# Two-layer hybrid diffusion step on one Trainium2 core: the instruction order made by the scheduler's detailed timeline instead of its plain one

## The chip, the cores and the metric

One core of one Trainium2 chip runs the whole program. The metric is device time in microseconds (us), as the median of several runs. Engines are named as in the profile: PE (TensorE), PEld (its weight load), DVE (VectorE), ACT (ScalarE), POOL (GpSimd), SP (SyncE, which issues most transfers).

## What is computed

Two layers (DEPTH = 2), width D = 2048, on 128 context and 128 latent tokens. Cut to what matters, one layer is:

```
m = adaLN(c)                      # shift, scale, gate: 2 x 3 vectors, from ada_w
h = norm(x) * scale + shift
u = h @ w_in                      # one product for all three head groups
oA = windowed attention(u)        # 12 heads, sink, context keys
oB = Hyena convolution by FFT(u)
oC = RWKV-7, forward and backward(u)   # 12 heads, decay, delta rule, chunked
x = x + gate * norm([oA, oB, oC] @ w_out)
h = norm(x) * scale' + shift'
x = x + gate' * norm(relu(h @ w1)^2 @ w2)
```

Weights are fp32. Each one is split into a high and a low part, and a product is three matmuls (high x high, low x high, high x low).

## The kernel before

**The main work** streams weights. `wload` (L208) issues a transfer on SP (L218), ACT casts the high part (L219), DVE subtracts for the low part (L220). `ws` (L482) then issues matmuls 256 columns wide (L495, L498, L499), and `as_` (L505) matmuls 512 columns wide (L514, L517, L518; 256 wide for the attention values). The input product is `ws` for RWKV and Hyena and `as_` for attention; the output product `w_out` is `as_`; the MLP uses both.

**The modulation work** ("ADA" below) makes the adaLN vectors: transfer L369, small matmuls L374, 16 to a piece. The first vectors are made in a boot stretch (L329 to L344), the others between main products.

**The side work** of the mixer is written as generators that the main loops advance (`Side`, L130): attention, Hyena, and RWKV in two batches (0 and 1) of three blocks of two heads each. For one batch the steps follow one another:

1. `rwkv_stage1` (L803): per block a transpose of the values (L814), small products (L820 to L850), transposes (L880), 32 matmuls of line L904, products L914 to L925, transposes L933, whose result POOL stores (L938).
2. `rwkv_invert` (L947): eight loads on SP of the stored matrices (L956, tile rX), a triangular inversion on DVE of 30 steps (L964, L965), a copy and a store (L971, L977).
3. `rwkv_stage2` (L981): loads the inverse (L985), then seven half-steps of 24 small matmuls each (L1003, L1001, L1003, ...), each followed by an L1007 pair on DVE, or by an L1009 copy on DVE and an L1011 copy on ACT; then L1018 to L1027.
4. `rwkv_out` (L1033): group norm and output transposes (L1061).

**What sets the order.** The program's own order is a priority. A scheduler of the library then puts the instructions of each engine into the order in which they go on the chip; it simulates when an instruction could start. In the kernel before it uses its plain timeline. Every engine runs its list in that fixed order: an instruction that isn't ready holds up all behind it on its engine. `w_out` runs in three phases over the heads (L1098 on), attention's and Hyena's heads first, RWKV's batch 0 and then batch 1 last. So the mixer ends with: batch 1's chain, the last phase, the residual and the norm (L1205).

## Time and profile before

| | |
|---|---|
| median of 3 runs | 2949.42 us (2944.27 to 2960.29) |
| profiled execution, its own time | 2948.62 us |
| its span | 2946.8 us |
| PE busy | 2833.7 us (96%) |
| PEld, DVE, ACT, POOL busy | 79%, 56%, 42%, 6% |
| bytes moved | 654.56 MB, mean 222 GB/s |
| boot; mixer 0; MLP 0; mixer 1; MLP 1 begin at about | 0; 140; 770; 1620; 2210 us |

PE is busy nearly all the time. What is left to win or lose is the time in which PE waits, and the time in which it runs at the lower of its two clocks: busy time there counts as busy too, so the granted clock (1.00 is 2.4 GHz, 0.50 is 1.2 GHz) must be read beside it. Stretches are therefore read one by one, not by the average.

### The profile page before, as it was taken

To read this page: it belongs to the slowest core of one execution; us is meant where nothing else is said; L and a number is where in the kernel's file an instruction comes from. 1 tells how busy PE (TensorE), PEld (TensorE's weight loads), DVE (VectorE), ACT (ScalarE), POOL (GpSimd) and SP (SyncE) were. 2 spreads that over 40 slices of the span, in tenths; PEclk is the share of its full clock that TensorE was granted. 3 is DMA by queue.
4 is the path that set the end of the run, shared out by engine and by line. 5 is a ranking of instruction groups with operands and counts; after the bars stand their busy time and mean duration, and the time that the engine had idled before them with its cause. 6 is when DMAs were issued, how large, how long until landed. Compare 5 with 4: busy or idle time off the path is not lost.

```text
span 2946.8 us, 47852 instructions
## 1 busy us (share of the span) xinstructions
PE 2833.7 (96%) x19163; PEld 2318.8 (79%) x19163; DVE 1651.4 (56%) x2627; ACT 1230.8 (42%) x1870; POOL 177.5 (6%) x368
## 2 busy tenths in 40 slices
PE   6899999999899999999999999999879999999998
PEld 2586787767797797897876978887669989889896
DVE  1356666776654344444446576776775545545555
ACT  2354345434543343343335454453355444444343
POOL 0011101201000000000000111011000000000000
PEclk9999899999999999999999998998889999999999
DMA  9985575477888888888898744533455666666674
GB/s 337 333 296 185 188 253 157 137 258 275 296 280 288 275 287 274 299 283 281 284 334 274 232 135 114 147 93 95 138 189 170 188 187 186 186 187 186 188 240 150
DMA packets 326057, 654.56 MB, mean 222 GB/s; under 512 B 48581, under 2 KB 86030, under 8 KB 325707
## 3 DMA queue, kind: packets, MB, share of 16 engines
q1 hardware_dynamic: 311328, 610.88, 64.0%
q0 software_dynamic: 12928, 36.98, 3.8%
q10 hardware_dynamic: 1579, 3.64, 0.3%
q8 instruction: 150, 2.46, 0.3%
q14 instruction: 72, 0.59, 0.1%
HBM read 632.21 MB, written 19.20 MB: 221 GB/s over the span
## 4 chain that ended last, share of the span: by engine, by line
PE 86%; DVE 5%; DMA 5%; ACT 2%; issue 1%; SPq 0%; POOL 0%; DVEq 0%; ACTq 0%; POOLq 0%
PE mm L495 12%; PE mm L499 12%; PE mm L498 12%; PE mm L514 11%; PE mm L517 11%; PE mm L518 11%; PE ada L374 5%; PE sm L904 2%; DMA wa<-in_ada_w_dram 2%; PE sm L925 1%; PE sm L1003 1%; DVE wl L220 1%; PE sm L1018 1%; PE sm L1001 1%; DMA wr<-in_ada_w_dram 1%
## 5 line engine op out<-in xcount | busy, mean ns | idle before, releaser
L220 DVE TENSOR_TENSOR wl<-wr,wh 128x1024 fp32r<-128x1024 f32 (+1 forms) x784 | 928.1, 1185 | 931.2 <-ACT wh L219 910.0
L219 ACT CAST wh<-wr 128x1024 fp32r<-128x1024 f32 (+1 forms) x784 | 796.5, 1017 | 1169.3 <-PE mm L498 545.6
L495 PE MATMUL mm<-acth,wh 128*128 128x256 f32 (+1 forms) x3200 | 914.4, 286 | 11.5 <-ACT acth L476 9.2
L499 PE MATMUL mm<-acth,wl 128*128 128x256 f32 (+1 forms) x3200 | 907.1, 283 | 2.4 <-DVE wl L220 2.4
L498 PE MATMUL mm<-actl,wh 128*128 128x256 f32 (+1 forms) x3200 | 907.5, 284 | 0.3 <-DVE actl L477 0.3
L495 PEld LDWEIGHTS mm<-acth,wh 128*128 128x128 f32 (+1 forms) x3200 | 605.2, 189 | 56.3 <-issue 23.8
L499 PEld LDWEIGHTS mm<-acth,wl 128*128 128x128 f32 (+1 forms) x3200 | 605.2, 189 | 8.3 <-DVE wl L220 3.4
L498 PEld LDWEIGHTS mm<-actl,wh 128*128 128x128 f32 (+1 forms) x3200 | 605.4, 189 | 3.9 <-issue 2.5
L517 PE MATMUL mm<-wl,fh 128*128 128x512 f32 x1024 | 408.0, 398 | 0.3 <-DVE wl L220 0.3
L514 PE MATMUL mm<-wh,fh 128*128 128x512 f32 x1024 | 406.6, 397 | 0.0
L518 PE MATMUL mm<-wh,fl 128*128 128x512 f32 x1024 | 402.4, 393 | 0.0
L514 PEld LDWEIGHTS mm<-wh,fh 128*128 128x128 f32 x1024 | 191.8, 187 | 67.6 <-ACT wh L219 10.9
L518 PEld LDWEIGHTS mm<-wh,fl 128*128 128x128 f32 x1024 | 192.3, 188 | 45.7
L517 PEld LDWEIGHTS mm<-wl,fh 128*128 128x128 f32 x1024 | 192.4, 188 | 43.8 <-DVE wl L220 0.8
L374 PE MATMUL ada<-wa,cs 128*32 128x512 f32 x1280 | 180.6, 605 | 9.2 <-DMA wa<-in_ada_w_dram 9.1
L514 PE MATMUL mm<-wh,osh 128*128 128x512 f32 x256 | 108.8, 425 | 3.4 <-ACT osh L1172 3.4
L517 PE MATMUL mm<-wl,osh 128*128 128x512 f32 x256 | 105.0, 410 | 3.4 <-DVE wl L220 3.4
L518 PE MATMUL mm<-wh,osl 128*128 128x512 f32 x256 | 103.0, 402 | 0.0
L374 PEld LDWEIGHTS ada<-wa,cs 128*32 128x32 f32 x1280 | 35.3, 109 | 84.9 <-issue 54.2
L904 PE MATMUL sm<-rZR,rKB 64*128 64x256 f32 x384 | 83.8, 456 | 0.7 <-DVE rLA L908 0.3
L514 PE MATMUL mm<-wh,acth 128*128 128x512 f32 (+1 forms) x192 | 74.8, 389 | 0.0
L517 PE MATMUL mm<-wl,acth 128*128 128x512 f32 (+1 forms) x192 | 69.1, 360 | 0.0
(323 smaller groups left out, 2598.2 us busy)
## 6 DMA issues: line engine op xcount, KB each, us to landing
wr<-in_mlp_w_dram SPq DMA_DIRECT2D x512, 512.0 KB
wa<-in_ada_w_dram SPq DMA_DIRECT2D x352, 512.0 KB
wr<-in_w_in_dram SPq DMA_DIRECT2D x96, 512.0 KB
wr<-in_w_in_dram SPq DMA_DIRECT2D x112, 384.0 KB
wr<-in_w_out_dram SPq DMA_DIRECT2D x64, 512.0 KB
wr<-in_ada_w_dram SPq DMA_DIRECT2D x32, 512.0 KB
gb<-gate POOLq DMA_DIRECT2D x16, 512.0 KB, 8.9
xd<-acc SPq DMA_DIRECT2D x24, 256.0 KB
```

Of the source, the lines that this page charges most:

```text
L219: nc.scalar.copy(hi, raw)
L220: nc.vector.tensor_sub(lo, raw, hi)
L374: nc.tensor.matmul(ps[32 * j:32 * j + 32, :], lhsT=self.cs[:, kk, :], rhs=w[2 * (kk - k + 1) + j // 2][:, 512 * (j % 2):512 * (j % 2) + 51 ...
L495: m = nc.tensor.matmul(o, lhsT=h, rhs=hh, start=(k == 0 and b % 2 == 0), stop=False, skip_group_check=True)
L498: nc.tensor.matmul(o, lhsT=h, rhs=hl, start=False, stop=False, skip_group_check=True)
L499: nc.tensor.matmul(o, lhsT=lw, rhs=hh, start=False, stop=(k == KT - 1), skip_group_check=True)
L514: m = nc.tensor.matmul(o, lhsT=hh, rhs=hi[:, kk, :], start=first, stop=False)
L517: nc.tensor.matmul(o, lhsT=hh, rhs=lo[:, kk, :], start=False, stop=False)
L518: nc.tensor.matmul(o, lhsT=hl, rhs=hi[:, kk, :], start=False, stop=last)
L904: nc.tensor.matmul(ps[h][:, i * 256:(i + 1) * 256], lhsT=KB[hs, d, g, i, :], rhs=ZR[hs, d, g, :, :].rearrange("p i t -> p (i t)"), start=T ...
L925: nc.tensor.matmul(o[:, 64 * h:64 * h + 64], lhsT=R.MA[d][h][:, 0:128] if i == 0 else MY[h][:], rhs=vT[:, g, 64 * h:64 * h + 64], start=fi ...
L1001: nc.tensor.matmul(o, lhsT=LA[d][:, gh, qs[d]], rhs=G[:, d, gh, :], start=True, stop=True)
```

## The change

The context that holds the scheduler is opened with a flag: the scheduler then times the instructions with its detailed timeline of engines and DMAs. Nothing else is edited.

```
-    with _tile.TileContext(nc) as tc:
+    with _tile.TileContext(nc, schedule_with_timeline_sim=True) as tc:
```

Every engine has the same compute instructions before and after; their order differs in the boot, in both mixers and in the residual between, and is the same on PE in both MLPs. On PE 2748 of 15617 rows of the order move. In the rows below a name is a tile (the number is its instance), `<-` stands before what is read, and `x2` counts equal neighbours. The three places are these.

**PE, layer 1, RWKV batch 1, from the first block to the second in stage 1.** The tiles `mm` are of the main input product. Before:

```order
L814 MATMUL sm_19059<-const_66,ru_v_17922 128x128 x2
L499 MATMUL mm_19097<-acth_14714,wl_19100 128x256
L495 MATMUL mm_19097<-acth_14714,wh_19099 128x256
L820 MATMUL sm_19064<-rtw_15195,rup_18776 128x256 x2
L828 MATMUL sm_19071<-rad_15196,rup_18778 128x256 x2
L845 MATMUL sm_19124<-rinv_2844_18774,const_66 128x256
L850 MATMUL sm_19128<-rrk_19057,const_66 128x256
L498 MATMUL mm_19097<-actl_14715,wh_19099 128x256
L499 MATMUL mm_19097<-acth_14714,wl_19100 128x256
L495 MATMUL mm_19097<-acth_14714,wh_19099 128x256
```

Now:

```order
L814 MATMUL sm_19059<-const_66,ru_v_17922 128x128 x2
L925 MATMUL sm_19011<-rvT_18785,rMY_19008 128x64
L820 MATMUL sm_19064<-rtw_15195,rup_18776 128x256 x2
L828 MATMUL sm_19071<-rad_15196,rup_18778 128x256 x2
L845 MATMUL sm_19124<-rinv_2844_18774,const_66 128x256
L850 MATMUL sm_19128<-rrk_19057,const_66 128x256
L880 MATMUL sm_19181<-const_66,rkf_19155 128x128 x2
L904 MATMUL sm_19212<-rZR_19149,rKB_19150 128x256
L904 MATMUL sm_19213<-rZR_19149,rKB_19150 128x256
```

The main matmuls that stood between the small ones of this block have all gone ahead of it; the three blocks of this batch now follow each other with no main matmul between.

**DVE, layer 1, the start of the first inversion.** L708 to L718 are attention's softmax, tile rX is what the inversion works on. Before:

```order
L715 TENSOR_TENSOR ast_17290<-ast_17290 128x4
L716 RECIPROCAL ast_17290<-ast_17290 128x4
L718 TENSOR_SCALAR ape_17294<-ape_17294,ast_17290 128x128 x4
L964 TENSOR_TENSOR rkt_17015<-rX_16860 112x30
L965 TENSOR_TENSOR rX_16860<-rX_16860,rkt_17015 112x30
```

Now:

```order
L669 TENSOR_TENSOR att_16980<-aqk_15976,const_66 128x16x16 x4
L672 TENSOR_TENSOR arq_16979<-arq_16979,att_16980 128x1024
L220 TENSOR_TENSOR wl_17450<-wr_17448,wh_17449 128x768
L220 TENSOR_TENSOR wl_17493<-wr_17491,wh_17492 128x768
L964 TENSOR_TENSOR rkt_17015<-rX_16860 112x30
L965 TENSOR_TENSOR rX_16860<-rX_16860,rkt_17015 112x30
L964 TENSOR_TENSOR rkt_17018<-rX_16860 112x58
L708 TENSOR_REDUCE ast_17223<-sm_17218 128x4
```

The inversion has moved ahead of the first two groups of the softmax, and the rotation of the queries (L669, L672) still stands ahead of it.

**SP, layer 0, RWKV batch 1, the loads of the inversion.** `L218` rows are weights of `w_out`. Now (before, the two rX rows were one, `x8`):

```order
L956 DMA rX_5619<-rdin_4681 12x32x32 x4
L218 DMA wr_6135<-in_w_out_dram 128x2x512
L218 DMA wr_6167<-in_w_out_dram 128x2x512
L218 DMA wr_6195<-in_w_out_dram 128x2x512
L218 DMA wr_6237<-in_w_out_dram 128x2x512
L956 DMA rX_5619<-rdin_4681 12x32x32 x4
```

Four weight loads now stand between the two halves of the eight loads; in the other three inversions there are two, two and four. In the boot the same kind of move stands on SP: two modulation tiles (L369) are now issued ahead of the last four boot weights (L329), where none was.

## Rows read from the trace of the kernel before

**Rows 1.** The page: the chain of waits that ended last, share of the span by engine.

```profile
PE 86%; DVE 5%; DMA 5%; ACT 2%; issue 1%; SPq 0%; POOL 0%; DVEq 0%; ACTq 0%; POOLq 0%
```

**Rows 2.** Stretches: length, busy us (instructions) of PE, PEld, DVE, ACT, POOL, clock, DMA.

```profile
0.00:140.00 140.00, 105.55 (x642) 57.52 (x643) 32.50 (x73) 37.74 (x72) 4.68 (x14) 0.94 0.94 336
140.00:717.00 577.00, 561.86 (x4149) 428.58 (x4148) 377.70 (x779) 242.12 (x456) 78.30 (x162) 0.97 0.66 220
770.00:1576.00 806.00, 806.00 (x5277) 662.23 (x5277) 371.22 (x389) 307.34 (x342) 12.52 (x23) 1.00 0.85 286
1620.00:2171.00 551.00, 528.90 (x3897) 441.10 (x3890) 380.15 (x773) 241.71 (x453) 70.13 (x146) 0.94 0.47 142
```

**Rows 3.** Single lines, layer 1: counts, duration ns, first and last start, forms.

```profile
L933 PE MATMUL sm<-const,rLA x12: 270/273/278, 1735.6 to 1789.6; 128*128 128x128 f32 x12
L956 SPq DMA_DIRECT2D rX<-rdin x8: 290/425/438, 1790.6 to 1797.3; - x8
L964 DVE TENSOR_TENSOR rkt<-rX x30: 183/350/410, 1815.4 to 1858.1; 112x30 f32<-112x30 f32 x2, 112x58 f32<-112x58 f32 x2, 112x84 f32<-112x84 f32 x2, 112x108 f32<-112x108 f32 x2
L1003 PE MATMUL sm<-rG,rXT x112: 213/214/239, 1877.3 to 1899.7; 32*32 32x64 f32 x112
L814 PE MATMUL sm<-const,ru_v x6: 272/272/273, 1950.5 to 2018.0; 128*128 128x128 f32 x6
L933 PE MATMUL sm<-const,rLA x12: 271/276/422, 1977.0 to 2043.9; 128*128 128x128 f32 x12
L964 DVE TENSOR_TENSOR rkt<-rX x30: 183/342/408, 2064.1 to 2101.0; 112x30 f32<-112x30 f32 x2, 112x58 f32<-112x58 f32 x2, 112x84 f32<-112x84 f32 x2, 112x108 f32<-112x108 f32 x2
L1003 PE MATMUL sm<-rG,rXT x192: 213/215/310, 2111.2 to 2152.7; 32*32 32x64 f32 x192
```

**Rows 4.** Stretches of full main work (256 wide, then 512), columns as in 2.

```profile
1840.00:1850.00 10.00, 10.00 (x87) 10.00 (x86) 9.69 (x21) 4.96 (x7) 0.00 (x0) 1.00 0.69 193
2600.00:2610.00 10.00, 10.00 (x44) 8.04 (x43) 4.02 (x4) 4.19 (x4) 0.00 (x0) 1.00 0.64 180
```

**Rows 5.** The chain in order of time: start, us, what; one piece of modulation work.

```profile
776.05 1.85 PE ada L374 x16
```

**Rows 6.** DVE in order of time near 1806 us: start, us, what, idle before.

```profile
1805.93 1.43 DVE L669 TENSOR_TENSOR att<-aqk,const 128x256 f32<-128x256 f32 x4 [5.72 <-PE sm L693]
```

**Rows 7.** Groups by line, 2100 to 2171 us: busy, mean ns, idle before and releaser.

```profile
L1007 DVE TENSOR_TENSOR rG<-rG,sm 32x256 f32<-32x256 f32 x18 | 7.5, 417 | 4.4 <-PE sm L1001 4.0
L1009 DVE COPY rG<-sm 32x256 f32<-32x256 f32 x12 | 5.0, 420 | 11.4 <-PE sm L1003 11.2
```

**Rows 8.** Single lines, layer 0, columns as in 3.

```profile
L933 PE MATMUL sm<-const,rLA x12: 270/273/277, 251.8 to 310.9; 128*128 128x128 f32 x12
L964 DVE TENSOR_TENSOR rkt<-rX x30: 182/352/409, 338.0 to 380.4; 112x30 f32<-112x30 f32 x2, 112x58 f32<-112x58 f32 x2, 112x84 f32<-112x84 f32 x2, 112x108 f32<-112x108 f32 x2
L1003 PE MATMUL sm<-rG,rXT x192: 213/214/239, 392.7 to 448.8; 32*32 32x64 f32 x192
L1003 PE MATMUL sm<-rG,rXT x192: 213/214/239, 649.0 to 695.1; 32*32 32x64 f32 x192
```

**Rows 9.** Line L904, two blocks of layer 1, columns as in 3.

```profile
L904 PE MATMUL sm<-rZR,rKB x32: 375/377/482, 1747.3 to 1758.1; 64*128 64x256 f32 x32
L904 PE MATMUL sm<-rZR,rKB x32: 376/632/793, 1995.1 to 2013.6; 64*128 64x256 f32 x32
```

**Rows 10.** Stretches in which PE waits, columns as in 2.

```profile
330.00:350.00 20.00, 14.58 (x76) 11.77 (x73) 14.15 (x49) 9.23 (x30) 0.94 (x1) 0.59 0.17 50
1800.00:1820.00 20.00, 14.93 (x96) 12.60 (x95) 9.51 (x36) 6.43 (x24) 0.00 (x0) 0.71 0.20 74
1990.00:2010.00 20.00, 17.70 (x68) 11.57 (x66) 13.01 (x30) 4.68 (x9) 0.31 (x1) 0.65 0.28 95
2100.00:2120.00 20.00, 15.06 (x99) 10.74 (x99) 9.94 (x20) 7.41 (x14) 0.17 (x1) 0.71 0.56 149
```

**Rows 11.** Waits of the DMA queue of SP: us in total, times, longest.

```profile
SPq L218 <- DVE wl L220: 1592.9, 615, 15.9
```

## The prediction

> **What bounds the kernel now.** I read the chain of waits first, then the stretches, then single lines in order of time. The chain runs over PE for 86% of the span [rows 1]: the reader is to see that no transfer and no other engine sets the time as a whole, so a new order can win only where PE waits or runs at its lower clock. The stretches say where that is [rows 2]. MLP 0 has PE busy for all of its 806 us at full clock, and its order is not touched: nothing is to be had there. Mixer 0 has PE busy for 561.86 of 577 us at a mean clock of 0.97, mixer 1 for 528.90 of 551 us at 0.94. So PE waits 15.1 us and 22.1 us there, and the boot waits for its transfers (DMA share 0.94, PE busy 105.55 of 140 us). Those three are the only places where something is left, and all three are reordered. A measurement can tell about 0.5% from no change here, 14.7 us; the median is 2949.42 us and the profiled execution 2948.62 us, so the sum below is made against the latter, which is 0.8 us lower.
>
> Inside the mixers the rule is plain. PE does its main matmuls at a fixed pace and the RWKV chain of each batch runs beside them. The mixer cannot end before batch 1's chain has. Where the order puts main matmuls ahead of a chain step, the chain starts later; where it leaves none beside a chain step, PE waits. The change does the first early and so the second late.
>
> **Prices.** In a full stretch PE does 86 to 87 of the 256-wide matmuls in 10 us, 0.116 us each, and 44 of the 512-wide, 0.23 us each [rows 4]. Modulation work is 16 matmuls in 1.85 us, 0.116 us each [rows 5], or 0.23 us for a row of two.
>
> **Layer 1, batch 0.** Counting PE's two orders, the last L933 of batch 0 now has 153 more `ws` matmuls and 54 more 256-wide `as_` matmuls ahead of it: 207 x 0.116 = 24.0 us. It started at 1789.6 us [rows 3], in a stretch where PE did not wait; so now at about 1814. From there to the first L1003 the kernel took 87.7 us (1877.3) [rows 3]. In that time the loads of rX were issued by 1797.3, but the inversion began only at 1815.4 [rows 3], since DVE stood before an attention step that waited 5.7 us for PE [rows 6] and then before the softmax. The inversion itself took 42.7 us, with some 13 subtractions L220 between its steps. Now the inversion stands ahead of the softmax and has about half as many L220 inside. I count 10 us from L933 to the landed loads, 30 us for the inversion (30 steps of two instructions of about 0.34 us are 20 us, plus six or seven L220 of 1.2 us) and the 19.2 us that lay behind it: 60 us. So the first L1003 comes at 1874, 3 us earlier than before, with 72 `ws` matmuls (8.4 us) fewer done. By the first L814 of batch 1 the new order has 174 more main matmuls ahead, which is 246 more in between than before: 28.5 us. It goes from 1950.5 [rows 3] to about 1976, **25 us late**.
>
> **Layer 1, batch 1.** From the first L814 to the last L933 it took 93.4 us (2043.9) [rows 3]. The main work inside changes by 150 `ws` matmuls less (17.4 us) and 82 512-wide ones more (18.9 us), nearly nothing, but it no longer lies between the three blocks; they follow bare. I take the same 93 us. From the last L933 to the first L1003 it took 67.3 us (2111.2) [rows 3], with 22 us of main work in it that is now ahead; bare it needs the 60 us worked out above: 7 us back. The lateness is 18 us there, and the main work done by then equals that of before. In stage 2 the last three half-steps now have no main work beside them. What shows bare in one is an L1007 pair or an L1009 with its ACT copy, about 0.83 us [rows 7]: 2.5 us, with 0 and 6 as bounds (6 if each of the nine groups in them also shows a queue turn of about 0.4 us, what DVE lost per group in its 4.4 us of idle time over 18 instructions [rows 7]). Part of the start is made good, since the 5.1 us in which PE waited from 1800 to 1820, at a clock of 0.71 [rows 10], go. That is counted in the 60 us already, but the clock is not: 0.29 of 15 us, 4 us. **Layer 1: 18 + 2.5 - 4 = +17 us**; bounds 5 and 25.
>
> **Layer 0.** By the same count the last L933 of batch 0 (310.9) [rows 8] has 213 more 256-wide main matmuls and 16 modulation rows ahead, 28.4 us. The inversion began 27 us after it (338.0) [rows 8] and the first L1003 came at 392.7, 81.8 us after it [rows 8]; at 60 us it comes 7 us late. By the first L1003 of batch 1 (649.0) [rows 8] 48 512-wide matmuls and 63 modulation rows are ahead in all, 25.5 us, 15 us of them since the last point: 22 us late. Behind that, 25.5 us less is left to do. If all of it comes off the end, layer 0 is 4 us faster; if none, 22 us slower. Stage 2 needs some of it as cover: seven half-steps of some 2 us of turns, 14 us, so 11.5 us come off: +10. The low clock from 330 to 350 us (0.59 with 14.58 us busy [rows 10]) goes as well and gives back 4 to 6 us. **Layer 0: +6 us**; bounds -4 and +22.
>
> **Boot and the rest.** Two modulation tiles now stand on SP ahead of the last four boot weights. The stretch moves 336 GB/s [rows 2], and a tile is 0.52 MB, so 1.6 us each: up to 3 us late. Against it, 14 modulation rows (3.2 us) fill time in which PE waited. I take 0, bounds -3 and +13 (if all eight tiles issued early delay it). The MLPs keep their order on PE: 0. What hides their weight loads is PE work that is not moved; DVE and ACT are under 60% there.
>
> **Sum.** 2948.6 + 17 + 6 + 0 = 2971.6, so **2972 us**, 0.8% slower.
>
> One row speaks on the clock in the bare blocks. The 32 matmuls of L904 took 10.8 us in a block at full clock and 18.5 us in a block during the stretch from 1990 to 2010 us, where PE waited and the granted clock was 0.65 [rows 9, 10]: PE that had waited was granted 1.2 GHz. I charge nothing for this, because one of batch 1's three blocks ran slow before as well and the others had lulls. The Trainium skill, page "TensorE: Matmul & The Clock Gate", section "HAM oscillation - how this bites in real kernels", says that a PE which waits between groups of matmuls is throttled again at each of them; by that rule all three bare blocks would run slow, and the sum would be about 2987 us. The trace agrees for one block and not for the other.
>
> **The rivals.**
> *Faster.* The waits of the mixers vanish and no new ones come: the inversion starts 14 us earlier, attention no longer makes PE stand, and the chain's head start outweighs the work put ahead. The four waiting stretches hold 5.4, 5.1, 2.3 and 4.9 us of waiting, and their busy time at clocks of 0.59 to 0.71 loses another 6.0, 4.3, 6.2 and 4.4 us [rows 10]: together 38.6 us, so 2910 us. For it: all four are at the places that the new order fills or empties, and the scheduler's aim is the time of just these engines. Against it: the counts above put the chain later, and the end of a mixer hangs on the chain. It decides if batch 1's last L933 comes no more than 5 us late. Partly reached, it gives up to 2934.
> *No change.* The parts cancel: cover lost in batch 1 equals cover gained in batch 0, so about 2949 us. PE's work is the same, its waits are 37 us of two mixers, and shifting them is no gain or loss by itself.
> *Slower still.* The low clock takes two more bare blocks, 2 x 7.7 us [rows 9], 2987 us; or the second half of an rX load stands on SP behind four weight loads whose buffers come free late, for up to the longest such wait, 15.9 us [rows 11], 2988 us; both, 3003 us.
> That the change does nothing is excluded: the rows of PE's order differ.
>
> **How the numbers follow.** My forecast (about 2955 to 2985 us) has 0.40, slower still 0.16, no change 0.22, faster 0.22. Bounds of 0.5% are 2934.7 and 2964.2 us. Of the forecast 0.07 lies under 2964.2. That gives faster 0.22, same 0.29, slower 0.49. For 8 in 10 the range reaches down into the faster rival, to 2920, leaving its better half (about 0.11), and up to 3003, leaving some 0.07. The likeliest case's own range is 2955 to 2985 us.
>
> **What would show it.** Right: the last L933 of layer 1's batch 0 near 1814 us and its L964 within 12 us of it; the L814 of batch 1 some 25 us late; PE waiting in the blocks and the inversion of batch 1; both MLPs of unchanged length. Wrong: L933 of batch 1 within 5 us of before or PE at full clock throughout mixer 1 (the faster rival); L904 blocks of 18 us in all three bare blocks, or rX loads that land over 10 us apart (slower still).

## The result, and the profile after

The change made the kernel slower: 3101.24 us (median of 4 runs, 3096.23 to 3105.71) against 2948.24 us, a ratio of 1.0508 with a 95% interval of 1.0484 to 1.0533. The forecast was 2972 us with a range of 2920 to 3003. The side was right, the size was not: 153 us came where 23 were forecast.

Two statements ahead of the prediction have to be put right first. A piece of modulation work is eight matmuls, each with two records in the trace, and not 16 matmuls. And PE's order is the same in MLP 1 only, behind the transposes of its norm. In MLP 0 the main matmuls keep their order among themselves, but the modulation matmuls (L374) have moved among them. The prediction priced that stage at nothing.

The page of the changed kernel:

```profile
span 3102.6 us, 47878 instructions
...
PE 2919.1 (94%) x19163; PEld 2343.6 (76%) x19163; DVE 1651.1 (53%) x2627; ACT 1231.5 (40%) x1870; POOL 179.0 (6%) x368
...
PE 87%; DVE 5%; DMA 5%; ACT 2%; issue 1%; SPq 0%; POOL 0%; DVEq 0%; ACTq 0%; POOLq 0%
```

PE's chain share is 87% after 86% [rows 1]: the share tells nothing of the loss. PE is busy for 85 us more with the same instructions, and it waits for 70 us more. So both must be looked for stage by stage. The stretches below end at the first transpose (L466) of each norm, for the kernel before (boot, mixer 0, MLP 0, mixer 1, MLP 1; columns as in rows 2):

```profile
0.00:140.00 140.00, 105.55 (x642) 57.52 (x643) 32.50 (x73) 37.74 (x72) 4.68 (x14) 0.94 0.94 336
140.00:749.00 609.00, 589.61 (x4274) 445.22 (x4272) 404.97 (x823) 262.06 (x501) 82.23 (x170) 0.97 0.66 222
749.00:1588.00 839.00, 832.60 (x5442) 679.41 (x5441) 396.54 (x446) 328.94 (x395) 13.54 (x25) 1.00 0.85 288
1588.00:2201.00 613.00, 576.41 (x4170) 479.12 (x4169) 428.09 (x862) 284.17 (x536) 72.83 (x151) 0.94 0.50 151
2201.00:2946.80 745.80, 729.49 (x4640) 657.56 (x4640) 389.26 (x424) 317.86 (x367) 4.22 (x8) 0.99 0.62 185
```

and the same for the changed kernel:

```profile
0.00:140.00 140.00, 103.83 (x626) 55.77 (x628) 31.16 (x70) 35.70 (x68) 1.48 (x8) 0.84 0.92 335
140.00:808.00 668.00, 626.21 (x4344) 462.49 (x4341) 406.24 (x828) 265.63 (x504) 86.29 (x176) 0.95 0.66 221
808.00:1703.00 895.00, 881.63 (x5445) 678.11 (x5445) 396.71 (x447) 328.23 (x395) 13.57 (x25) 0.99 0.80 267
1703.00:2357.00 654.00, 577.08 (x4114) 489.57 (x4112) 427.25 (x861) 283.90 (x536) 73.40 (x151) 0.90 0.43 128
2357.00:3102.60 745.60, 730.31 (x4640) 657.66 (x4640) 389.74 (x426) 318.03 (x368) 4.25 (x8) 0.99 0.61 184
```

Three stages lose, each in its own way. Mixer 0 is 59 us longer: 37 us of it PE is busy, 22 us it waits. MLP 0 is 56 us longer, and 49 us of that PE is busy with almost the same number of matmuls; the other 7 us go with one wait of 11.0 us for the norm at its end (1702.6 us), where the kernel before had modulation work. Mixer 1 is 41 us longer, and all but 1 us of that is waiting. Its busy time is equal because two things cancel: 56 records of L374 (8.9 us) have left this stage, and the other matmuls are busy 9.6 us longer, at a granted clock of 0.90 for 0.94. MLP 1 has the same length.

**What PE is busy with.** The chain in order of time shows it. In the kernel before, a stretch of MLP 0 (start, us, what; x16 is a whole piece):

```profile
1010.16 0.24 PE mm L518
1010.40 1.85 PE ada L374 x16
1012.25 0.43 PE mm L514
```

In the changed kernel, the same work in the same stage:

```profile
1023.65 0.99 PE ada L374 x6
1024.64 0.43 PE mm L517
...
1027.17 0.24 PE mm L518
1027.41 0.97 PE ada L374 x2
1028.38 0.42 PE mm L514
1028.81 0.98 PE ada L374 x4
```

A piece of 16 records takes 1.85 us. A part of two, of four and of six takes 0.97, 0.98 and 0.99 us. Parts of eight take 1.00 us, and the two of ten take 1.83. So up to eight records the number of matmuls in a part hardly matters; the number of parts does. Measured from main matmul to main matmul, less the usual pitch (0.23 us for the 512-wide ones, 0.12 for the 256-wide), a part of up to eight records costs 1.08 us and a piece of 16 costs 1.95. MLP 0 has 110 groups of L374 now and had 47; by that measure they come to 135 us for 90. Its L374 groups by line (busy, mean ns of one, idle before), before and then after:

```profile
L374 PE MATMUL ada<-wa,cs 128*32 128x512 f32 x766 | 96.7, 603 | 4.1 <-DMA wa<-in_ada_w_dram 4.1
```

```profile
L374 PE MATMUL ada<-wa,cs 128*32 128x512 f32 x768 | 134.3, 602 | 0.0
```

The mean of one is 603 and 602 ns, so this column shows nothing; the busy column does (37.6 us more), since the matmuls of one group overlap (16 records of 0.6 us in 1.85 us) and there are more groups now.

**What PE waits for in mixer 1.** Groups by line, first before, then after:

```profile
L495 PE MATMUL mm<-acth,wh 128*128 128x256 f32 (+1 forms) x576 | 166.3, 289 | 2.5 <-ACT acth L476 2.2 <-ACT wh L219 0.3
...
L1003 PE MATMUL sm<-rG,rXT 32*32 32x64 f32 x384 | 16.8, 228 | 1.6 <-DMA rXT<-rdout 1.6
...
L880 PE MATMUL sm<-const,rkf 128*128 128x128 f32 x24 | 5.4, 310 | 4.5 <-ACT rkf L874 4.4
```

```profile
L495 PE MATMUL mm<-acth,wh 128*128 128x256 f32 (+1 forms) x576 | 166.8, 290 | 11.7 <-DVE ru_k L528 11.7
...
L1003 PE MATMUL sm<-rG,rXT 32*32 32x64 f32 x384 | 15.5, 218 | 22.3 <-DMA rXT<-rdout 20.8 <-DVE rG L1007 1.5
...
L880 PE MATMUL sm<-const,rkf 128*128 128x128 f32 x24 | 5.6, 328 | 14.6 <-ACT rkf L874 14.6
```

These three waits grew by 9.2, 20.7 and 10.1 us, 40 us together, which is the stage's loss. The timeline of PE and of the inversion's end in the changed kernel shows the longest of them (in brackets the wait and who ended it):

```profile
2243.96 0.39 PE L640 MATMUL sm<-const,hyb 128*128 128x128 f32 x2
...
2256.93 1.03 DVE L971 COPY rXo<-rX 48x1024 f32<-48x1024 f32 x1
2258.27 3.17 SPq L977 DMA_DIRECT2D rdout<-rXo  x8
2261.67 1.86 SPq L985 DMA_DIRECT2D rXT<-rdout  x2
2264.62 0.81 PE L1003 MATMUL sm<-rG,rXT 32*32 32x64 f32 x6 [20.28 <-DMA rXT<-rdout]
```

PE had nothing left to do beside the end of batch 1's inversion. The wait of 11.7 us is one wait, at 1977.4 us: a main product needs the PSUM tile that the convolution L528 must read first, and L528 stands on DVE behind the first part of batch 0's inversion and attention's softmax. Of the 14.6 us, 10.0 are one wait, at 2149.2 us, in the second block of batch 1, whose new order the section on the change shows.

**Mixer 0.** L374 by line, before and after:

```profile
L374 PE MATMUL ada<-wa,cs 128*32 128x512 f32 x456 | 74.5, 609 | 5.1 <-DMA wa<-in_ada_w_dram 5.0
```

```profile
L374 PE MATMUL ada<-wa,cs 128*32 128x512 f32 x496 | 100.7, 639 | 17.9 <-DMA wa<-in_ada_w_dram 17.7 <-DVE mod L355 0.3
...
L466 PE MATMUL sm<-const,xn 128*128 128x128 f32 x2 | 0.7, 434 | 13.4 <-DVE rs L448 13.4
```

26 us more of busy PE with 40 records more, 12.7 us more of waiting for the modulation's loads, and 13.4 us before the norm, where the kernel before had modulation work as filler. The rest is the boot's, since its end counts here: the first L814 came 9.3 us late.

### The profile page after: what moved, and what is told of

It is laid out like the page before. It is cut to its first block, busy times and chain, and to the rows that moved or that the text cites. A ratio compares the mean times of both kernels' runs of the same rounds, so it can differ in the third digit from the quotient of the medians.

```text
span 3102.6 us, 47878 instructions
## 1 busy us (share of the span) xinstructions
PE 2919.1 (94%) x19163; PEld 2343.6 (76%) x19163; DVE 1651.1 (53%) x2627; ACT 1231.5 (40%) x1870; POOL 179.0 (6%) x368
## 4 chain that ended last, share of the span: by engine, by line
PE 87%; DVE 5%; DMA 5%; ACT 2%; issue 1%; SPq 0%; POOL 0%; DVEq 0%; ACTq 0%; POOLq 0%
PE mm L495 12%; PE mm L498 12%; PE mm L499 12%; PE mm L517 11%; PE mm L514 11%; PE mm L518 11%; PE ada L374 6%; PE sm L904 3%; DMA wa<-in_ada_w_dram 2%; PE sm L925 1%; PE sm L1018 1%; PE sm L1003 1%; DMA wr<-in_w_in_dram 1%; DMA wr<-in_ada_w_dram 1%; DVE wl L220 1%
## 5 line engine op out<-in xcount | busy, mean ns | idle before, releaser
L495 PE MATMUL mm<-acth,wh 128*128 128x256 f32 (+1 forms) x3200 | 912.5, 285 | 20.4 <-DVE ru_k L528 13.5
L495 PEld LDWEIGHTS mm<-acth,wh 128*128 128x128 f32 (+1 forms) x3200 | 605.0, 189 | 53.3 <-issue 30.9
L517 PE MATMUL mm<-wl,fh 128*128 128x512 f32 x1024 | 414.6, 405 | 0.5 <-DVE wl L220 0.2
L374 PE MATMUL ada<-wa,cs 128*32 128x512 f32 x1280 | 239.9, 618 | 17.9 <-DMA wa<-in_ada_w_dram 17.7
L374 PEld LDWEIGHTS ada<-wa,cs 128*32 128x32 f32 x1280 | 39.1, 110 | 112.8 <-issue 58.8
L904 PE MATMUL sm<-rZR,rKB 64*128 64x256 f32 x384 | 99.6, 445 | 2.8 <-ACT rKBt L882 1.4
L907 DVE COPY_PREDICATED rMA<-masks,sm 128x256 f32<-128x256 uint8 x96 | 42.5, 443 | 81.6 <-PE sm L904 81.2
L904 PEld LDWEIGHTS sm<-rZR,rKB 64*128 64x128 f32 x384 | 58.9, 205 | 25.3 <-issue 9.7
```

The lines of the kernel that those rows point to most:

```text
L374: nc.tensor.matmul(ps[32 * j:32 * j + 32, :], lhsT=self.cs[:, kk, :], rhs=w[2 * (kk - k + 1) + j // 2][:, 512 * (j % 2):512 * (j % 2) + 51 ...
L495: m = nc.tensor.matmul(o, lhsT=h, rhs=hh, start=(k == 0 and b % 2 == 0), stop=False, skip_group_check=True)
L517: nc.tensor.matmul(o, lhsT=hh, rhs=lo[:, kk, :], start=False, stop=False)
L904: nc.tensor.matmul(ps[h][:, i * 256:(i + 1) * 256], lhsT=KB[hs, d, g, i, :], rhs=ZR[hs, d, g, :, :].rearrange("p i t -> p (i t)"), start=T ...
L907: nc.vector.copy_predicated(R.MA[d][h], mk[d], ps[h][:, 0:256])
```

## The experiments

Most of these hold an engine to a given order. The edit is one call behind `build()`; the table is a list of numbers and differs from run to run. The edges put the instructions of one engine in a row and add no semaphore. No run holds a kernel to its own order throughout, so the price of the edges alone isn't shown; but e8 and e11, which hold PE nearly to its old order, took 2945 and 2946 us, so it can't be large.

```
             Kern(tc, es, A, O).build()
+            force_order(tc, nc)
+def force_order(tc, nc):
+    raw = zlib.decompress(base64.b85decode(_ORDER))
+    pe = [i for i in nc.cur_bb.bb.instructions if type(i).__name__ == "InstMatmult"]
...
+        tc.add_manual_dep(pe[at], prev.name, mybir.DependencyInfo(mybir.DependencyClass.NoSync, mybir.DependencyReason.DATA), reason="order")
```

All runs in one table (us; stages of the profiled execution from the same bounds as above, so that a late boot counts in mixer 0; ratios against runs of the kernel before that were made with each experiment, medians 2946.51 to 2949.81). The profiled executions of e2 (3061.52 us) and e10 (3065.68 us) were the longest of theirs, so their stages hold 15 and 9 us more than the medians.

| run | timeline | held | mixer 0 | MLP 0 | mixer 1 | median | ratio, 95% interval |
|---|---|---|---|---|---|---|---|
| before | plain | | 609 | 839 | 613 | 2948.24 | |
| changed | detailed | | 668 | 895 | 654 | 3101.24 | 1.0484 to 1.0533 |
| e1 | plain | PE as changed | 694 | 900 | 651 | 3141.24 | 1.0622 to 1.0668 |
| e2 | detailed | PE as before | 672 | 843 | 658 | 3046.10 | 1.0306 to 1.0346 |
| e3 | detailed | PE as changed, pieces gathered | 669 | 842 | 656 | 3058.84 | 1.0345 to 1.0390 |
| e4 | plain | | 658 | 961 | 619 | 3125.27 | 1.0575 to 1.0609 |
| e5 | detailed | e3, `w_out` held back | 661 | 843 | 655 | 3050.67 | 1.0316 to 1.0368 |
| e6 | detailed | e5, tail filled | 671 | 842 | 661 | 3061.85 | 1.0354 to 1.0396 |
| e7 | plain | PE as before, `w_out` ahead | 621 | 839 | 636 | 2989.05 | 1.0110 to 1.0148 |
| e8 | plain | PE as before, attention spread | 602 | 838 | 615 | 2945.23 | 0.9961 to 0.9995 |
| e9 | detailed | PE, DVE as before | 644 | 842 | 622 | 2994.87 | 1.0111 to 1.0183 |
| e10 | plain | PE as before, DVE as in e2 | 670 | 842 | 664 | 3056.74 | 1.0329 to 1.0401 |
| e11 | plain | PE as before, pieces gathered | 603 | 840 | 615 | 2946.19 | 0.9969 to 1.0002 |
| e12 | plain | e11, attention of layer 0 spread | 602 | 840 | 612 | 2944.10 | 0.9974 to 1.0016 |
| e13 | detailed | PE, DVE, SP as before | 615 | 838 | 620 | 2961.89 | 1.0035 to 1.0086 |
| e14 | plain | PE as changed in MLP 0 | 636 | 897 | 605 | 3027.38 | 1.0218 to 1.0295 |

**e1 and e2: whose order is it?**

> The plain timeline orders DVE, ACT, SP and POOL, and PE is held to the order that the detailed timeline gave it. Theory (PE's order alone makes the loss): 3085 to 3115 us, L374 busy near 240 us as in the changed kernel. Rival (the orders of DVE and SP, with the loads of the inversion parted, make it): 2940 to 2970 us. Both share it: in between, and the distance from either end says how much is whose.

> The detailed timeline orders DVE, ACT, SP and POOL, and PE is held to the order of the kernel before. Theory (PE's order alone makes the loss): 2935 to 2965 us, L374 busy near 181 us. Rival (the other engines' orders make it): over 3050 us. If the rX loads that are parted on SP cost what the prediction's rival gave them, it is 2964 us or more with longer gaps between L933 and L964.

Measured 3141 us, above the theory's interval, and 3046 us, just under the rival's. Neither theory holds alone. MLP 0's loss comes with PE's new order in e1 and is nearly gone with the old one in e2 (900 and 843 us, for 839), so that part is PE's order. But both mixers lose with either: with PE's new order and the other engines ordered for it by the plain timeline, and with PE's old order and the others ordered by the detailed one. In mixer 1 of e2 the long waits at L1003 and L495 are gone, and the one at L880 is longer:

```profile
L880 PE MATMUL sm<-const,rkf 128*128 128x128 f32 x24 | 6.6, 366 | 19.5 <-ACT rkf L874 19.5
```

19.5 us in place of 4.4, the longest single one 7.1 us. One block shows why: the DVE subtractions between its L814 and its L880, for the kernel before from 1737.3 to 1746.8 us and then for e2 from 1816.2 to 1827.9:

```profile
L220 DVE TENSOR_TENSOR wl<-wr,wh 128x1024 fp32r<-128x1024 f32 x1 | 1.2, 1225 | 3.8 <-ACT wh L219 3.8
```

```profile
L220 DVE TENSOR_TENSOR wl<-wr,wh 128x1024 fp32r<-128x1024 f32 x3 | 3.7, 1219 | 4.7 <-ACT wh L219 4.7
```

Two more subtractions of 1.2 us stand in front of the serial steps of the block, and the block's first half takes 11.7 us for 9.5. In the other eleven blocks of e2 there are one to three more. Waiting isn't all of the loss: with the same matmuls PE is busy for 597.29 us in mixer 1 of e2, for 576.41 in the kernel before, at a granted clock of 0.90 for 0.94.

**e3: the pieces put together again.**

> The changed kernel with PE's order held as it is, but for the modulation matmuls: the eight of each piece stand together where the last of them stood. Theory (a parted piece costs PE about 1.08 us for each part of up to four matmuls, against 1.95 us for a whole one of eight, 49 us in MLP 0 and some 60 to 75 us in all): 3025 to 3050 us, MLP 0 back to about 840 us. Rival (the parts only fill time in which PE would wait, and MLP 0 is longer for late weights): over 3085 us and MLP 0 still near 890 us.

Measured 3058.84 us, 42 us back, all of it in MLP 0 (842 for 895 us). L374 there in e3:

```profile
L374 PE MATMUL ada<-wa,cs 128*32 128x512 f32 x768 | 95.9, 603 | 3.7 <-DMA wa<-in_ada_w_dram 3.7
```

95.9 us, as before the change. The theory of the parts is shown for MLP 0. It missed by 9 us in all, since mixer 0 got nothing: PE was busy 11 us less there and waited 13 us more. In a stage with waits a parted piece is partly filler.

**e4: parting alone, under the plain timeline.**

```
-                if len(w) == 4:
-                    for kk in (k - 1, k):
-                        for j in range(4):
-                            nc.tensor.matmul(...
+                for j in (2 * h, 2 * h + 1):
+                    nc.tensor.matmul(ps[32 * j:32 * j + 32, :], lhsT=self.cs[:, k, :], ...
```

> The kernel before with the plain timeline, but each modulation tile's two matmuls are issued when that tile comes, so that PE has 284 parts of two matmuls in place of 61 pieces of eight. Theory (a part costs about 1.08 us however few its matmuls): 303 parts by 1.08 us are about 325 us against 175 us, so 120 to 150 us more, 3065 to 3100 us, L374 busy above 270 us. Rival (the price in the changed kernel is not of the parting): 2940 to 2975 us.

Measured 3125.27 us, 176 us more: dearer than the 120 to 150 forecast, and the rival falls. MLP 0 takes 961 us, 122 more. By the measure above its 179 parts between main matmuls come to 193 us, 1.08 us each, for 90 us before, and the main matmul behind each part is some 0.1 us longer as well. Mixer 0 is 49 us longer. The scheduler orders this program anew, so other instructions can have moved with the parts.

**e5, e6 and e7: the cover of the second inversion.** Cover is main work that PE can do while a chain runs on other engines.

> As e3 (3059 us), and in each mixer 106 main matmuls, 22 us, that the kernel before has behind the last L933 of RWKV's batch 1 are held there again (82 of w_out, 24 of the input product). Theory (the 20.3 us in which PE waits for the second inversion of layer 1 is the cover that these were): that wait falls under 5 us, mixer 1 shortens by 12 to 20 us, mixer 0 by 0 to 8 us since its wait there was 2.5 us, 3030 to 3048 us. Rival (the wait only moves ahead, to the blocks from which they are taken): 3052 to 3066 us, with the waits of L880 for L874 longer by as much.

> As e5, and 48 modulation matmuls of layer 0 stand behind the last matmul of w_out, where the kernel before has them. Theory (the 13.4 us in which PE waits there for the norm's L448 is work that was filler before): that wait falls to 3 us or less and the time by 5 to 10 us against e5. Rival (those pieces filled waits as long where they stood): within 4 us of e5.

> The kernel before with the plain timeline, and one thing of the new order: in each mixer the same 106 main matmuls, 22 us, stand ahead of the last four L933 of batch 1. Theory (cover taken from the second inversion shows as a wait there): a wait of 10 to 22 us before the first L1003 of batch 1 in each layer, 2975 to 2995 us. Rival (the chain has room, or what was lost is won ahead): 2943 to 2958 us.

e5 is a miss for the theory: 3050.67 us lies between the two intervals, and mixer 1 takes 655 us for e3's 656. Its waits:

```profile
L1003 PE MATMUL sm<-rG,rXT 32*32 32x64 f32 x384 | 15.8, 220 | 15.6 <-DMA rXT<-rdout 14.1 <-DVE rG L1007 1.5
...
L880 PE MATMUL sm<-const,rkf 128*128 128x128 f32 x24 | 6.1, 355 | 25.1 <-ACT rkf L874 25.1
```

Against e3 (22.3 and 14.6 us) the wait at the inversion's end fell by 6.7 us and the wait of the blocks grew by 10.5. The 22 us of main work only changed which of two holes they fill. e6 fell too: the 13.4 us before the norm went, and 3061.85 us is no gain on e5, because PE then waited in four places there for the modulation's loads, 10.6 us together; its rival, within 4 us of e5, isn't met either. e7 is in the theory's interval of times (2989.05 us, 12 us more in mixer 0 and 23 in mixer 1), but not where it said. PE does not wait at L1003; it waits where Hyena's last transforms need DVE, L639 in mixer 1 of e7:

```profile
L639 PE MATMUL sm<-const,hya 128*128 128x128 f32 x16 | 5.0, 439 | 13.6 <-DVE o L642 13.1 <-DVE hyt L628 0.5
```

So 22 us of main work put ahead of the chain cost 12 and 23 us in the kernel before. In the changed kernel there is more than one hole, and one piece of cover can't fill them all.

**e8, e11 and e12: is any gain left?**

> The kernel before with the plain timeline, and one other thing of the new order: between the first L693, L705 and L725 of attention 43 and 57 main matmuls are placed, taken from right behind. Theory (the gain that the prediction saw is there, and the order hid it): the waits from 330 to 350 and from 1800 to 1820 us and their half clock go, 5 us of waiting and 4 to 6 us of clock each, 2925 to 2942 us. Rival (the inversion behind the softmax on DVE starts later by as much): 2944 to 2965 us.

> The kernel before with the plain timeline and PE held to its own order, but for the modulation matmuls: the eight of each piece stand together where the last of them stood, 78 groups in place of 102. Theory (each group saved is worth up to 1.08 us, most of them in mixer 0): 2930 to 2943 us. Rival (the parts fill waits there, as e3's mixer 0 had it): 2945 to 2955 us.

> As e11, and the main matmuls of e8 between attention's first steps, in layer 0 alone, where e8 won 7 us. Theory: the gains add, 6 to 8 us less than e11. Rival (they use the same waits): within 3 us of e11.

e8 measured 2945.23 us, a ratio of 0.9978 (0.9961 to 0.9995): a gain of 0.2%, all of it in mixer 0 (602 for 609 us), none in mixer 1. It is the fastest that this study shows to differ from the kernel before, but its time lies in the rival's interval. The 24 groups saved in e11 gave back 6 us of mixer 0 in the profiled execution, but its ratio of 0.9985 has 1 in its interval, and e12 adds nothing that can be told from no change. Both came out as their rivals had it.

**e9, e10 and e13: which engine, with PE's order held.**

> As e2 (the detailed timeline with PE held to the order of the kernel before, 3046 us), and DVE held to the order of the kernel before too; ACT, SP and POOL stay with the detailed timeline. Theory (e2's loss is DVE's order: three weight subtractions L220 instead of one stand between L814 and L880 in each block of stage 1, PE waits 2 to 7 us for L874 there and its clock falls each time): 2943 to 2970 us. Rival (the casts on ACT or the issue order on SP make it): over 3010 us.

> The kernel before with the plain timeline, PE held to its own order, and DVE held to the order that it had in e2. Theory (DVE's order alone is enough): 3020 to 3055 us, with the waits of L880 for L874 back. Rival (it takes ACT's and SP's order as well): 2945 to 2985 us.

e10: DVE's order alone, with everything else left to the plain timeline, gives 3056.74 us, no less than e2. It is enough. (It is the order that DVE has in e2; the changed kernel's own order of DVE wasn't tried by itself.) L880 in mixer 1 of e10, and then its mixers 0 and 1 as stretches:

```profile
L880 PE MATMUL sm<-const,rkf 128*128 128x128 f32 x24 | 6.5, 362 | 17.8 <-ACT rkf L874 17.8
...
140.00:810.00 670.00, 625.35 (x4304) 470.35 (x4302) 407.51 (x824) 262.95 (x501) 85.92 (x176) 0.91 0.62 206
1652.00:2316.00 664.00, 595.62 (x4171) 491.79 (x4172) 429.05 (x865) 284.43 (x537) 72.90 (x151) 0.90 0.46 139
```

Against the kernel before PE waits 25 and 32 us longer in them, and it is busy 36 and 19 us longer with 30 records and one record more. So nearly half of this loss is no waiting: PE does the same matmuls more slowly, at a granted clock of 0.91 and 0.90 for 0.97 and 0.94.

e9: with DVE's order put back, mixer 1 returns to 622 us and L880 waits 7.2 us there; but 2994.87 us lies between theory and rival, and 35 us are lost in mixer 0. Its first L814 came at 239.6 us, for 219.4 in the kernel before.

> As e9 (2995 us), and SP too is held to the order of the kernel before, so that only ACT and POOL stay with the detailed timeline. Theory (what is left in e9 is SP's order, first of all the boot, where modulation tiles stand ahead of weights and the first L814 came at 239.6 us against 219.4): the first L814 within 4 us of 219.4, 2943 to 2972 us. Rival (ACT's order): the first L814 early, but the time still 2980 us or more.

e13 measured 2961.89 us: SP's order was worth 33 us of what e9 still lost, 29 of them in mixer 0. The first L814 came at 233.2 us, not within 4 us of 219.4, so that detail was wrong. What is left, 14 us, goes with ACT's or POOL's order, 6 us in mixer 0 and 7 in mixer 1; which of them wasn't tried. So PE's, DVE's and SP's old order together give back 139 of the 153 us. The shares don't add up one by one: DVE's order is worth 51 us when it is put right in e2 and 110 us when it alone is changed in e10.

**e14: MLP 0 alone.**

> The kernel before with the plain timeline and PE held to its own order up to the end of mixer 0, then to the order of the changed kernel through MLP 0 and the norm behind it, then to its own again. Theory (the parted modulation pieces of MLP 0 are by themselves worth what e3 gave back, 52 us): MLP 0 near 890 us, 2990 to 3010 us, both mixers as before. Rival (they only cost with the loads of the detailed timeline): under 2965 us.

MLP 0 took 897 us, as expected, with the loads of the plain timeline. The total of 3027.38 us is above the interval, since the join put modulation pieces at the end of mixer 0 (636 for 609 us), where PE is busy 17 us longer and waits 10 us more; mixer 1, with 55 records fewer, is 8 us shorter. L374 in MLP 0 of e14:

```profile
L374 PE MATMUL ada<-wa,cs 128*32 128x512 f32 x768 | 138.4, 608 | 4.9 <-DMA wa<-in_ada_w_dram 4.8
```

## Why the prediction was wrong

**MLP 0: "The MLPs keep their order on PE: 0".** This step failed outright, and it is the largest error in one stage, 56 us of the 130 missed. The order of main matmuls is unchanged there, and I took that for the whole order. e3 and e14 show that the parted pieces cost it, by PE's order alone.

**The price of modulation work, "0.116 us each".** It was read from a whole piece of 16 records in 1.85 us [rows 5] and holds only for that. A part of two records costs nearly as much as one of eight. With 1.08 us for a part and 1.95 for a whole piece, the new groups of MLP 0 come to the 45 us above, most of what PE is busy longer there (49 us).

**Layer 1: +17 us, measured +41.** The single lines of the changed kernel's layer 1, which answer to [rows 3]:

```profile
L933 PE MATMUL sm<-const,rLA x12: 271/279/421, 1862.5 to 1941.3; 128*128 128x128 f32 x12
...
L1003 PE MATMUL sm<-rG,rXT x192: 211/214/239, 1997.8 to 2051.7; 32*32 32x64 f32 x192
...
L814 PE MATMUL sm<-const,ru_v x6: 272/272/421, 2099.7 to 2162.6; 128*128 128x128 f32 x6
...
L933 PE MATMUL sm<-const,rLA x12: 272/278/421, 2132.7 to 2208.6; 128*128 128x128 f32 x12
...
L1003 PE MATMUL sm<-rG,rXT x192: 211/214/309, 2264.6 to 2304.0; 32*32 32x64 f32 x192
```

The way was right, the sizes were not. All numbers here have the 115 us taken off by which mixer 1 began later. The stretch from the last L933 to the first L1003 was put at 60 us and took 56.5 and 56.0 us. That step held, though the "some 13 subtractions" inside the first inversion were 18 in the kernel before (6 now). The last L933 of batch 0 came at 1826 us for the 1814 forecast. The 207 main matmuls counted ahead of it are there, and 56 records of L374 have gone; what the sum left out is the clock, granted at 0.94 from the stage's first L466 to this L933, for 0.99 before. L814 of batch 1 came 34 us late for 25. The failed term is "I take the same 93 us" for batch 1's stage 1: it took 108.9 us, though PE was busy for the same time as before (89.8 and 89.4 us). PE waited 10.0 us in the second block for a chain on DVE in which Hyena's convolutions stood between the block's own steps, and 6.7 us in the third for the casts of the input of `w_out` (L1172, L1173). And a chain that ends 38 us late at the first L1003 was not priced where it shows, as a wait of 20.3 us with nothing beside it. The attention wait of the kernel before [rows 6, 10] did go, as forecast; its place was taken by the 11.7 us for the convolution.

**Layer 0: +6 us, measured +59.** The lines that answer to [rows 8]:

```profile
L933 PE MATMUL sm<-const,rLA x12: 272/273/280, 277.1 to 359.8; 128*128 128x128 f32 x12
...
L1003 PE MATMUL sm<-rG,rXT x192: 214/214/238, 422.0 to 475.1; 32*32 32x64 f32 x192
...
L1003 PE MATMUL sm<-rG,rXT x192: 214/214/311, 716.6 to 748.9; 32*32 32x64 f32 x192
```

From the last L933 to the first L1003 of batch 0 it took 62.2 us for the 60 forecast; the L933 itself came 49 us late for 28, 9 us of it the boot's. The failed term is the "22 us late" at the first L1003 of batch 1: it was 68 us late. Behind it 9 us came off, near the 11.5 forecast. What was done early between the two first L1003 were modulation pieces, dearer by being parted: 232 records of L374 for 160, busy for 47.7 us in place of 26.1, and 12.5 us of waiting for their loads where there was none. They were then missing ahead of the norm, where PE waited 13.4 us. The prediction counted them at the price of whole pieces and as a share of cover in stage 2, not as the filler that they were.

**The boot: 0.** The changed kernel's first L814 came 9.3 us late (228.7 us), inside the bounds of -3 and +13.

**DVE's order** was weighed only at the start of the inversion. e10 shows that the order which DVE has in e2 is worth 110 us by itself with PE's old order: one to three more subtractions of weights stand in front of the chain in every block. In the changed kernel its part isn't shown so plainly: L880 waits 1.2 us in mixer 0 and 14.6 in mixer 1, and the longest of these waits stands behind Hyena's convolutions. I had looked for them inside the inversion, where there are fewer, and not in stage 1.

**The rivals.** The faster one fell; its part that is real is the 0.2% of e8. The bound it named ("batch 1's last L933 comes no more than 5 us late") was the right one to look at: it came 50 us late. On the low clock, the three blocks of batch 1 show L904 as follows in the changed kernel (the last view ends at 2200 us, with 27 of the 32):

```profile
L904 PE MATMUL sm<-rZR,rKB x32: 376/631/792, 2114.3 to 2129.9; 64*128 64x256 f32 x32
...
L904 PE MATMUL sm<-rZR,rKB x32: 376/376/792, 2149.8 to 2159.7; 64*128 64x256 f32 x32
...
L904 PE MATMUL sm<-rZR,rKB x27: 376/376/480, 2182.4 to 2199.8; 64*128 64x256 f32 x27
```

The median is at 1.2 GHz in the first (631 ns) and at 2.4 GHz in the two others (376 ns). Only the second was bare as the prediction had all three: 81 main matmuls ran in the first block ahead of its L904, and 82 in the third from 2171.3 us on. In the second the first eight took 631 to 792 ns right behind the wait of 10.0 us, and the others were fast; the granted clock was 0.56 from 2149.2 to 2153 us and 1.00 then. In the third it was 0.60 from 2171 to 2182 us, around waits of 4.8 and 1.9 us, and 1.00 when its L904 came. By the rule of the Trainium skill, page "TensorE: Matmul & The Clock Gate", section "HAM oscillation — how this bites in real kernels", a PE that waits between groups of matmuls is throttled again at each of them. The trace agrees: the clock fell at the waits of all three blocks (in the first to 0.72 from 2114 to 2124 us, where PE waited 1.7 us, and to 0.50 in the next 10 us). But three slow blocks, as the prediction had it by this rule, did not come of it: the clock was back before most of L904 in the second block and before all of it in the third. The mean clock of mixer 1 fell from 0.94 to 0.90, where the sum counted 4 us of gain by the clock. The rival of the parted rX loads on SP hardly cost: the inversions began 11 to 15 us after the last L933, where 10 were counted, not 16 us later.

## What to carry to other kernels

Small matmuls that share the array by column groups are cheap only as a run: before a scheduler is given freedom, tie such a run together, and price it by the number of its groups. When a schedule changes, compare the whole order of each stage, filler work too, and then read each engine's in-order queue for what now stands in front of the serial chain; e1 and e10 show that PE's order and an order of DVE are each enough to lose 38 to 85 us in a mixer where PE was busy for 94 or 97% of the time. Work that is pulled ahead of a chain is cover that is missing at its end, and moving one piece of it back (e5) fills one hole by opening another.

## What the runs showed of the hardware that was not expected

A group of the 32-column matmuls of L374 between full-width matmuls takes 0.97 to 0.99 us, whether it has two, four or six records, 1.00 us with eight, and the run of 16 takes 1.85 us. The first main matmul behind a group takes 0.42 or 0.43 us in place of 0.23 or 0.24 in either case. The Trainium skill, page "TensorE: Matmul & The Clock Gate", section "Part 3: Packing small matmuls — row/col tiling", has the time of a pack hardly grow with the number of its tiles. The trace agrees up to six records (0.02 us more than two); what a pack that is broken up loses is this case's number: MLP 0 of e4, with its pieces parted throughout, is 122 us longer.
